# Second RMS norm of a decoder block: 1/rms on quarters of the partitions, rows through temporaries, small additions and two weight splits on GpSimd

## The chip, the cores and the metric

One core of one Trainium2 chip runs the whole block in one launch. The metric is device time in microseconds (us), less is better. Engines are named as the profile names them: PE is TensorE, DVE is VectorE, ACT is ScalarE, POOL is GpSimd, SP is SyncE, which issues nearly all DMAs here.

## What is computed

A decoder block over 512 tokens of 1024 features: an adaLN norm, an input projection, windowed attention and a short convolution, an output projection, then a second adaLN norm and a mixture of single-neuron experts (PEER). Only the join between the last two matters here:

```python
    x = x + gate1[:, None, :] * (merged @ w_out[l])
    h2 = modulate(rmsnorm(x, norm2_g[l]), shift2, scale2)     # (.. * rsqrt(mean(x*x)+eps) * g) * (1+scale2) + shift2
    x = x + gate2[:, None, :] * peer(h2, peer_wq[l], peer_subkeys[l], peer_u[l], peer_v[l])
# peer():
    q = (xt @ wq).reshape(T, PEER_HEADS, 2, PEER_HALF)        # 16 query blocks of 128 columns
    sc = jnp.einsum('thpd,hpkd->thpk', q, subkeys)            # scores against 128 keys per block
    vals, ids = lax.top_k(sc, PEER_TOPK)
```

## The kernel before

The activations lie transposed, features on the partitions: `xT` is 8 blocks of 128 features by 512 tokens. Every matmul that must be exact runs as three: weight and input are split into a hi part (written by ACT, rounded) and a lo part (the rest, `raw` minus `hi`, by DVE or POOL), and `mm3` adds hi·hi, hi·lo and lo·hi (lines 200, 201, 202). A block of weights is one DMA of 512 KB into `raw` (5 buffers), one ACT copy to `hi` (line 176) and one subtraction to `lo` (line 177).

The framework orders each engine's instructions when the program is built; on the chip every engine, and SP with its DMAs, works through its own list in order, and an instruction that waits holds up what stands behind it on its engine. Memory of a pool that is closed is given to the next pools, and an instruction that writes there waits for the last readers.

The place of the change, in order:

- Output projection, blocks 0 to 7 (`out_half`): 24 matmuls a block into `py`. DVE adds each block to `xT` (line 544), ACT squares it (line 221), DVE adds the squares up (line 223). Between them DVE works off the last columns of the adaLN matrix (`more_ada`, line 213, from DMA loads of 512 KB into two buffers), the last weights' lo parts, and `s2`, 1 + scale2 times the norm's gain (line 554).
- Sum over features: two matmuls with a matrix of ones into the bank `ss2` (lines 551 and 552). Every row of the result is the same: the sum for each of 512 tokens, repeated on 128 partitions. `rstd` takes the square root on ACT (line 241) and the reciprocal on DVE (line 242), both on 128x512.
- `spill`: 32 transposes of the new `xT` (line 532) into eight banks `xt`; ACT copies each to a row tile `xn` (line 535), and SP writes it to memory (`x1s`, line 536). The `xn` have three buffers.
- `modulated`, for each of 8 blocks: DVE makes `f` = xT·s2·r2 (line 229), ACT makes `fH` (line 230), DVE makes `fL` (line 231). PE runs the first two query blocks (`early`, 48 matmuls into `pq`) as blocks come in. Their weights are the first two of sixteen; the lo parts of these two are DVE's, those of the other fourteen POOL's.
- Two small additions a block put shift2 into 256 columns of `f` on ACT (lines 590 and 592); 16 transposes (`pg`, line 593) then give the token-major `hN` and `h2N`.
- For each of 16 query blocks: ACT copies the query out (`qs`), SP loads 64 KB of keys (`sk`, line 729, three buffers), PE makes the scores (`psc`, line 738), DVE takes the top sixteen. On PE the scores of block n stand ahead of the matmuls of block n+2.

The temporaries `tmp` (f, sq, rstd and others) are one set of 9 buffers of 128x512. After the transposes their memory goes to the pools of the next stage, in which `sk` and `qs` lie.

Of the kernel before, what the change touches and what calls it, by code (L numbers as in the profile page):

```python
# [7 lines left out]
F32 = mybir.dt.float32  # L8
# [5 lines left out]
AF = mybir.ActivationFunctionType  # L14
# [4 lines left out]
P = 128  # L19
T = 512  # L20
NCH = 4
D = 1024
DC = 8
ND = 3
TD = ND * P
HT = 32
TU = TD - HT
# [11 lines left out]
EARLY = 2  # L39
# [50 lines left out]
def body(tc, p):  # L90
    nc = tc.nc
# [6 lines left out]
    cp, cp_s = pool("cp")  # L98
# [5 lines left out]
    rt, rt_s = pool("rt", side="right")  # L104
    R2 = dict(tag="s2", bufs=3)
    tp, tp_s = pool("tp", side="right")
    T2 = dict(tag="t2", bufs=9)
    xp, xp_s = pool("xp", side="right")

    def bank(name):  # L110
        return psm.tile([P, 512], F32, tag="m", name=name)
# [55 lines left out]
    mark = [None]  # L167
# [24 lines left out]
    def weights_of(src, by=nc.vector):  # L192

        h, l = parts(src.rearrange("p a b -> p (a b)"), by)
        return (lambda k: h[:, k * P:(k + 1) * P]), (lambda k: l[:, k * P:(k + 1) * P])
# [20 lines left out]
    def tmp(name):  # L216
        return tp.tile([P, T], F32, name=name, **T2)

    def squared(b, so_far=None):
        q = tmp("sq")  # L220
        nc.scalar.activation(q, b, AF.Square)
        if so_far is not None:
            nc.vector.tensor_add(q, q, so_far)
        return q
# [9 lines left out]
    def square(ps, b, i, n, w=None):  # L234
        q = tmp("sq")
        nc.scalar.activation(q, b, AF.Square)
        nc.tensor.matmul(ps, ones if w is None else w, q, start=(i == 0), stop=(i == n - 1))

    def rstd(ps, n):
        r = tmp("rstd")  # L240
        nc.scalar.activation(r, ps, AF.Sqrt, scale=1.0 / n, bias=eps)
        nc.vector.reciprocal(r, r)
        return r
# [284 lines left out]
    def spill(half, when):  # L528
        for c in range(NCH):
            ps = bank("xt")  # L530
            for i in range(4):
                after(nc.tensor.transpose(ps[:, i * P:(i + 1) * P], xT[:, 4 * half + i, c * P:(c + 1) * P], ident),
                      when)
            xn = rt.tile([P, 512], F32, name="xn", **R2)
            nc.scalar.activation(xn, ps, AF.Copy)
            nc.sync.dma_start(x1s[c][:, half * 512:(half + 1) * 512], xn)

# [10 lines left out]
        if b < 6:  # L548
            more_ada(3)
    sq = squared(xT[:, 6, :], sq)  # L550
    nc.tensor.matmul(ss2, ones, sq, start=True, stop=False)
    end = nc.tensor.matmul(ss2, ones, squared(xT[:, 7, :]), start=False, stop=True)
    nc.vector.tensor_add(mod[:, 24:48], mod[:, 24:48], ab[:, 24:48])
    nc.vector.scalar_tensor_tensor(s2, mod[:, 32:40], 1.0, S("n2g"), op0=OP.add, op1=OP.mult)
    a1_s.close()
# [16 lines left out]
    hx, hx_s = pool("hx")  # L572
    fH = hx.tile([P, DC, T], F32R, name="fH")
    fL = hx.tile([P, DC, T], F32R, name="fL")
    r2 = rstd(ss2, D)
    spill(0, end)
    spill(1, end)
    early = [(weights_of(p["wq"][b]), bank("pq")) for b in range(EARLY)]
    fs = []
    for k in range(DC):  # L580
        fs.append(modulated(fH[:, k, :], fL[:, k, :], xT[:, k, :], r2, s2[:, k:k + 1], mod[:, 24 + k:25 + k]))
# [2 lines left out]
    for r, (dst, cs) in enumerate(((hN, slice(TD - P, TD)), (h2N, slice(TD, T)))):  # L584
        pg = [bank("pg0"), bank("pg1")]
        for k in range(DC):
            b = mod[:, 24 + k:25 + k]
            f = fs[k]
            if r == 0:
                nc.scalar.activation(f[:, TD - P:TU].rearrange("p (q t) -> p q t", t=HT),  # L590
                                     f[:, None, TU:TD].to_broadcast([P, P // HT - 1, HT]), AF.Identity, bias=b)
                nc.scalar.activation(f[:, TU:T], f[:, TU:T], AF.Identity, bias=b)
            nc.tensor.transpose(pg[k // 4][:, (k % 4) * P:(k % 4 + 1) * P], f[:, cs], ident)
        for k in range(2):
            nc.scalar.activation(dst[:, k * 512:(k + 1) * 512], pg[k], AF.Copy)
    xp_s.close()
# [535 lines left out]
```

## Time and profile before

| | us |
|---|---|
| three runs | 1437.29, 1440.34, 1440.64 (median 1440.34) |
| the profiled execution, its own time | 1436.58 |
| its span in the trace | 1434.8 |
| PE busy | 1385.5 (97%) |
| DVE busy | 1229.3 (86%) |
| ACT busy | 616.0 (43%) |
| POOL busy | 442.7 (31%) |

The span runs from the first to the last instruction of the trace; the 1.8 us beside it are start and end. Busy shares are averages over stages with different limits, so the change, which touches some 30 us around 214 to 260 us, has to be read in that stretch: who waits for whom there, and what the delay of one engine does to the next. PE's granted clock is 0.994 of full speed over the whole span.

### The profile page before, as it was taken

The numbers are of one execution on the slowest core, as the hardware profiler recorded it, in microseconds if no ns is written. First come the engines' busy times: TensorE is split into PE (matmuls) and PEld (weight loads), VectorE is DVE, ScalarE is ACT, GpSimd is POOL, SyncE is SP. The second block draws the span as 40 slices with busy tenths as digits, with TensorE's granted clock in tenths as the row PEclk, the third lists the DMA queues.
The fourth block names the chain that finished last, engine by engine and source line by source line (L and its number), as shares of the span: only waits on it lengthen the run. The fifth ranks groups of instructions, "written<-read, shape, count | busy, mean of one in ns | idle before, by whom it ended". The sixth has DMA issues, their size and how long they took to land.

```text
span 1434.8 us, 21241 instructions
## 1 busy us (share of the span) xinstructions
PE 1385.5 (97%) x7696; PEld 1218.7 (85%) x7696; DVE 1229.3 (86%) x2253; ACT 616.0 (43%) x1041; POOL 442.7 (31%) x306
## 2 busy tenths in 40 slices
PE   6999998999997999999999999999999999999998
PEld 4676776888997999999888888889999998889997
DVE  7778988789999999997668989888889979898964
ACT  4524645544634556463433333333344324333431
POOL 0000001440112320510134444456556556565400
PEclk9999999999999999999999999999999999999999
DMA  8645545322687997998999999999999999999843
GB/s 282 213 150 195 190 131 197 99 86 78 212 290 236 383 372 262 348 356 324 365 333 374 405 396 379 396 370 360 360 362 396 383 357 343 367 339 390 318 147 132
DMA packets 134376, 418.80 MB, mean 292 GB/s; under 512 B 12800, under 2 KB 39552, under 8 KB 132736
## 3 DMA queue, kind: packets, MB, share of 16 engines
q1 hardware_dynamic: 92800, 266.45, 51.6%
q0 software_dynamic: 41472, 151.01, 27.9%
q8 instruction: 60, 0.98, 0.3%
q14 instruction: 44, 0.36, 0.1%
HBM read 375.77 MB, written 41.62 MB: 291 GB/s over the span
## 4 chain that ended last, share of the span: by engine, by line
PE 62%; DVE 20%; DMA 8%; issue 7%; POOL 1%; ACT 1%; SPq 0%; DVEq 0%; POOLq 0%; ACTq 0%
PE o L997 10%; PE o L998 10%; PE o L996 10%; PE pa L200 5%; PE pa L202 5%; PE pa L201 5%; DVE lo L177 4%; DMA row<-in_vL,eG 3%; DMA ada<-in_ada 2%; PE pq L202 2%; PE pq L201 2%; PE pq L200 2%; DVE B L946 2%; DVE ga L912 2%; PE pj L200 2%
## 5 line engine op out<-in xcount | busy, mean ns | idle before, releaser
L176 ACT ACTIVATE hi<-raw 128x1024 fp32r<-128x1024 f32 x298 | 312.1, 1053 | 286.8 <-issue 91.4
L177 DVE TENSOR_TENSOR lo<-raw,hi 128x1024 fp32r<-128x1024 f32 x284 | 345.2, 1218 | 31.9 <-ACT hi L176 31.1
L202 PE MATMUL pa<-h2H,lo 128*128 128x352 f32 x1024 | 329.8, 322 | 5.6 <-DVE lo L177 5.5
L200 PE MATMUL pa<-h2H,hi 128*128 128x352 f32 x1024 | 332.3, 325 | 2.2 <-ACT sp L620 2.2
L201 PE MATMUL pa<-h2L,hi 128*128 128x352 f32 x1024 | 328.9, 321 | 0.0
L997 PE MATMUL o<-lo,wwh 128*128 128x512 f32 x768 | 299.2, 390 | 0.9 <-DVE lo L177 0.9
L996 PE MATMUL o<-hi,wwh 128*128 128x512 f32 x768 | 299.6, 390 | 0.0
L998 PE MATMUL o<-hi,wwl 128*128 128x512 f32 x768 | 298.8, 389 | 0.0
L776 POOL DMA_INDIRECT row<-in_uR,eG x128 | 186.7, 1459 | 321.3 <-PE o L998 187.8
L776 POOL DMA_INDIRECT row<-in_vL,eG x128 | 178.8, 1397 | 136.8 <-PE o L998 65.6
L784 DVE SCALAR_TENSOR_TENSOR junk<-row,h2N 128x1024 bf16<-128x1024 f32 x128 | 153.8, 1220 | 64.9 <-DMA row<-in_uR,eG 64.4
L202 PEld LDWEIGHTS pa<-h2H,lo 128*128 128x128 f32 x1024 | 192.7, 188 | 6.9 <-DVE lo L177 6.8
L200 PEld LDWEIGHTS pa<-h2H,hi 128*128 128x128 f32 x1024 | 192.2, 188 | 4.9 <-ACT sp L620 2.7
L201 PEld LDWEIGHTS pa<-h2L,hi 128*128 128x128 f32 x1024 | 192.5, 188 | 2.2
L912 DVE SCALAR_TENSOR_TENSOR ga<-row,av,ga 128x1024 f32<-128x1024 f32 x127 | 162.8, 1282 | 29.8 <-DMA row<-in_vL,eG 28.7
L998 PEld LDWEIGHTS o<-hi,wwl 128*128 128x128 f32 x768 | 144.2, 188 | 30.0
L997 PEld LDWEIGHTS o<-lo,wwh 128*128 128x128 f32 x768 | 144.2, 188 | 29.7 <-DVE lo L177 1.6
L996 PEld LDWEIGHTS o<-hi,wwh 128*128 128x128 f32 x768 | 144.2, 188 | 28.3 <-issue 0.2
L176 ACT ACTIVATE wwh<-w 128x768 fp32r<-128x768 f32 x64 | 54.1, 846 | 168.0 <-DVE w L979 120.8
L177 POOL TENSOR_TENSOR lo<-raw,hi 128x1024 fp32r<-128x1024 f32 x14 | 33.8, 2413 | 288.3 <-ACT hi L176 288.3
L978 ACT ACTIVATE w<-G 128x32 f32<-128x32 f32 x128 | 22.3, 221 | 191.3 <-DVE wwl L177 182.8
L776 POOL DMA_INDIRECT row<-in_uR,eH x32 | 43.2, 1350 | 161.7 <-DVE junk L784 74.5
(266 smaller groups left out, 1896.1 us busy)
## 6 DMA issues: line engine op xcount, KB each, us to landing
raw<-in_uL SPq DMA_DIRECT2D x128, 512.0 KB, 6.0
raw<-in_vL SPq DMA_DIRECT2D x128, 512.0 KB, 6.5
Gd<-st SPq DMA_DIRECT2D x12, 2048.0 KB, 10.2
G<-Gd SPq DMA_DIRECT2D x16, 1536.0 KB, 12.5
ada<-in_ada SPq DMA_DIRECT2D x32, 512.0 KB, 4.3
Ad<-sp SPq DMA_DIRECT2D x34, 352.0 KB, 6.5
sp<-Ad SPq DMA_DIRECT2D x34, 352.0 KB, 6.6
raw<-in_w_in SPq DMA_DIRECT2D x18, 512.0 KB, 5.2
```

The lines of the kernel that those rows point to most:

```text
L176: nc.scalar.activation(h, f, AF.Copy)
L177: by.tensor_sub(l, f, h.bitcast(F32))
L200: nc.tensor.matmul(ps, wh(k), rh(k), start=(k == k0), stop=False)
L201: nc.tensor.matmul(ps, wh(k), rl(k), start=False, stop=False)
L202: mark[0] = nc.tensor.matmul(ps, wl(k), rh(k), start=False, stop=(k == k1))
L776: d = nc.gpsimd.indirect_dma_start(out=t, out_offset=None, in_=tab, in_offset=bass.IndirectOffsetOnAxis(ap=e, axis=0))
L784: return nc.vector.scalar_tensor_tensor(junk, t, 1.0, h, op0=OP.mult, op1=OP.mult, accum_out=a)
L912: nc.vector.scalar_tensor_tensor(ga, t, av[:, k:k + 1], ga, op0=OP.mult, op1=OP.add)
L946: nc.vector.tensor_mul(B.rearrange("p t (h a b) -> p t h a b", h=8, a=4), H[:, ts, :, None, :].to_broadcast(sh), L[:, ts, None].to_broadca ...
L996: nc.tensor.matmul(o, wh[:, cs], vh[:, hs], start=(j == 0), stop=False)
L997: nc.tensor.matmul(o, wh[:, cs], vl[:, hs], start=False, stop=False)
L998: last = nc.tensor.matmul(o, wl[:, cs], vh[:, hs], start=False, stop=(j == NJ - 1))
```

## The change

It does five things, all around the second norm.

1. `grouped`: the sum over features is made by 4 matmuls of 128 tokens with 32 columns of ones instead of one of 512 tokens with 128. Quarter c of the tokens lands on partitions 32c to 32c+31, in the same 128 columns. So the root and the reciprocal run on 128x128. `spread` brings it back by 4 matmuls into a PSUM bank `rr`, from which DVE's line 229 reads. On PE the first 16 transposes of `spill` stand between the sum and `spread`.
2. The `xn` rows come from the temporaries, which are 13 buffers instead of 9.
3. The lo parts of the first two query blocks' weights go from DVE to POOL.
4. The 16 small additions go from ACT to POOL.
5. The 16 transposes `pg` are tied behind the early query matmuls.

```diff
-    T2 = dict(tag="t2", bufs=9)
+    T2 = dict(tag="t2", bufs=13)
...
+    def grouped(ps, q, first, last):
+
+        for c in range(NCH):
+            end = nc.tensor.matmul(ps[32 * c:32 * c + 32, 0:P], ones[:, 0:32], q[:, c * P:(c + 1) * P], start=first,
+                                   stop=last)
+        return end
+
+    def grouped_root(ps, n):
+        r = cp.tile([P, P], F32, tag="r", name="r", bufs=1)
+        nc.scalar.activation(r, ps[:, 0:P], AF.Sqrt, scale=1.0 / n, bias=eps)
+        nc.vector.reciprocal(r, r)
+        return r
+
+    def spread(r):
+
+        ps = psa.tile([P, 512], F32, tag="a", name="rr")
+        for c in range(NCH):
+            nc.tensor.matmul(ps[:, c * P:(c + 1) * P], ident[:, 32 * c:32 * c + 1].to_broadcast([P, P]), r,
+                             start=True, stop=True)
+        return ps
...
-            xn = rt.tile([P, 512], F32, name="xn", **R2)
+            xn = tmp("xn")
...
-    nc.tensor.matmul(ss2, ones, sq, start=True, stop=False)
-    end = nc.tensor.matmul(ss2, ones, squared(xT[:, 7, :]), start=False, stop=True)
+    grouped(ss2, sq, True, False)
+    end = grouped(ss2, squared(xT[:, 7, :]), False, True)
...
-    r2 = rstd(ss2, D)
+    r2 = grouped_root(ss2, D)
     spill(0, end)
+    r2 = spread(r2)
     spill(1, end)
-    early = [(weights_of(p["wq"][b]), bank("pq")) for b in range(EARLY)]
+    early = [(weights_of(p["wq"][b], nc.gpsimd), bank("pq")) for b in range(EARLY)]
...
             if r == 0:
-                nc.scalar.activation(f[:, TD - P:TU].rearrange("p (q t) -> p q t", t=HT),
-                                     f[:, None, TU:TD].to_broadcast([P, P // HT - 1, HT]), AF.Identity, bias=b)
-                nc.scalar.activation(f[:, TU:T], f[:, TU:T], AF.Identity, bias=b)
-            nc.tensor.transpose(pg[k // 4][:, (k % 4) * P:(k % 4 + 1) * P], f[:, cs], ident)
+                nc.gpsimd.tensor_scalar_add(f[:, TD - P:TU].rearrange("p (q t) -> p q t", t=HT),
+                                            f[:, None, TU:TD].to_broadcast([P, P // HT - 1, HT]), b)
+                nc.gpsimd.tensor_scalar_add(f[:, TU:T], f[:, TU:T], b)
+            after(nc.tensor.transpose(pg[k // 4][:, (k % 4) * P:(k % 4 + 1) * P], f[:, cs], ident), mark[0])
```

How the built program stands at three places follows; lines of the changed kernel have its own numbers.

The first place is SP's list behind the writes of the rows (`raw` from `in_wq` is the weights of a later query block, `sk` the keys, the brackets name the engines and queues waited for). Before:

```order
L536 DMA x1s_1651<-xn_1978 128x512 [waits DMAHW2_49,Activation_49]
L729 DMA sk_2133<-in_sk 128x128 [waits DMAHW3_49,DVE_49,PE_49]
L729 DMA sk_2137<-in_sk 128x128 [waits DMAHW4_49]
L729 DMA sk_2167<-in_sk 128x128 [waits DMAHW5_49]
L181 DMA raw_2681<-in_wq 128x1024 [waits DMAHW6_49,Pool_49]
L729 DMA sk_2248<-in_sk 128x128 [waits DMAHW7_49,DMAHW3_49,PE_49]
```

The same place of the changed kernel:

```order
L557 DMA x1s_1651<-xn_1989 128x512 [waits DMAHW2_49,Activation_49]
L181 DMA raw_2692<-in_wq 128x1024 [waits DMAHW3_49,Pool_49]
L751 DMA sk_2144<-in_sk 128x128 [waits DMAHW4_49,DMAHW2_49,DMAHW5_49,DMAHW1_49,DMAHW6_49,DMAHW0_49,DMAHW7_49,DVE_49,PE_49]
L751 DMA sk_2148<-in_sk 128x128
L751 DMA sk_2178<-in_sk 128x128
```

The first three loads of keys have moved behind a load of weights. Of the two waits that the list shows: the weights' wait for POOL is for the lo part of query block 4 in both programs; the first keys' wait for PE is for `xt`, the last transpose of `spill`, before (and DVE's for the last `f`), and for the last of the 16 `pg` transposes now.

The second place is ACT's list behind the sum, `r` or `rstd` being the root. Before:

```order
L241 ACTIVATE rstd<-ss_1652,eps 128x512
L535 ACTIVATE xn<-xt 128x512 x5
L230 ACTIVATE fH<-f,mod 128x512
L535 ACTIVATE xn<-xt 128x512
L230 ACTIVATE fH<-f,mod 128x512 x2
L535 ACTIVATE xn<-xt 128x512 x2
```

Changed:

```order
L248 ACTIVATE r<-ss_1652,eps 128x128
L556 ACTIVATE xn<-xt 128x512 x8
L230 ACTIVATE fH<-f,mod 128x512 x8
L176 ACTIVATE hi<-raw 128x1024
L777 ACTIVATE h2H<-fH 128x352
```

All eight row copies now stand ahead of the first `fH`; there were five.

The third place is DVE's list while the last two blocks of the output projection finish, with the two lo parts that leave it:

```order
-L553 TENSOR_TENSOR mod<-mod,sm 128x24
-L177 TENSOR_TENSOR lo<-raw,hi 128x1024
-L554 SCALAR_TENSOR_TENSOR s_104<-mod,sm 128x8
-L177 TENSOR_TENSOR lo<-raw,hi 128x1024
-L544 SCALAR_TENSOR_TENSOR xT<-py,mod,xT 128x512
+L574 TENSOR_TENSOR mod<-mod,sm 128x24
+L575 SCALAR_TENSOR_TENSOR s_104<-mod,sm 128x8
+L565 SCALAR_TENSOR_TENSOR xT<-py,mod,xT 128x512
```

Nothing else moved there; on POOL four lo parts, those of query blocks 0 to 3, now come ahead of the 16 additions, and the lo part of block 4 behind them.

## Rows read from the trace of the kernel before

**Rows 1.** Busy time by stretch: us (instructions) of each engine, PE clock, DMA share, GB/s.
```profile
260.00:350.00 90.00, 89.44 (x457) 76.02 (x456) 81.77 (x503) 35.34 (x72) 25.26 (x11) 1.00 0.30 92
420.00:500.00 80.00, 72.14 (x571) 71.14 (x570) 80.00 (x179) 37.16 (x67) 20.50 (x15) 0.96 0.84 302
```

**Rows 2.** Timeline of PE, 218 to 270 us: start, us, instruction, idle before it.
```profile
230.93 0.39 PE L202 MATMUL py<-mH,lo 128*128 128x512 f32 x1
...
234.08 1.12 PE L552 MATMUL ss<-sq,ones 128*128 128x512 f32 x2 [0.20 <-ACT sq L221]
235.04 3.66 PE L532 MATMUL xt<-cst,xT 128*128 128x128 f32 x32
241.74 0.73 PE L200 MATMUL pq<-fH,hi 128*128 128x512 f32 x2 [3.04 <-ACT fH L230]
...
253.19 1.91 PE L593 MATMUL pg<-cst,f 128*128 128x128 f32 x16
254.93 1.06 PE L738 MATMUL psc<-sk,qs 128*128 128x128 f32 x8
```

**Rows 3.** Timeline of ACT, 200 to 285 us.
```profile
214.86 1.06 ACT L176 ACTIVATE hi<-raw 128x1024 fp32r<-128x1024 f32 x1 [1.65 <-PE py L201]
...
233.39 0.63 ACT L221 ACTIVATE sq<-xT 128x512 f32<-128x512 f32 x1 [0.47 <-DVE xT L544]
...
239.85 1.23 ACT L535 ACTIVATE xn<-xt 128x512 f32<-128x512 f32 x2 [2.46 <-DMA x1s<-xn]
240.97 0.71 ACT L230 ACTIVATE fH<-f,mod 128x512 fp32r<-128x512 f32 x1
...
252.47 1.06 ACT L176 ACTIVATE hi<-raw 128x1024 fp32r<-128x1024 f32 x1 [0.34 <-PE pq L201]
```

**Rows 4.** Timeline of DVE, 200 to 290 us.
```profile
216.53 1.23 DVE L213 SCALAR_TENSOR_TENSOR junk<-ada,cact 128x1024 bf16<-128x1024 f32 x1 [0.57 <-DMA ada<-in_ada]
...
223.19 0.74 DVE L544 SCALAR_TENSOR_TENSOR xT<-py,mod,xT 128x512 f32<-128x512 f32 x1
...
225.93 0.18 DVE L553 TENSOR_TENSOR mod<-mod,sm 128x24 f32<-128x24 f32 x1
226.02 1.22 DVE L177 TENSOR_TENSOR lo<-raw,hi 128x1024 fp32r<-128x1024 f32 x1
227.16 2.36 DVE L554 SCALAR_TENSOR_TENSOR s<-mod,sm 128x8 f32<-128x8 f32 x1
...
232.62 0.75 DVE L544 SCALAR_TENSOR_TENSOR xT<-py,mod,xT 128x512 f32<-128x512 f32 x1
```

**Rows 5.** Timeline of POOL, 210 to 300 us.
```profile
226.89 2.60 POOL L177 TENSOR_TENSOR lo<-raw,hi 128x1024 fp32r<-128x1024 f32 x1 [226.44 <-ACT hi L176]
233.00 2.35 POOL L177 TENSOR_TENSOR lo<-raw,hi 128x1024 fp32r<-128x1024 f32 x1 [3.51 <-ACT hi L176]
253.60 2.37 POOL L177 TENSOR_TENSOR lo<-raw,hi 128x1024 fp32r<-128x1024 f32 x1 [18.26 <-ACT hi L176]
```

**Rows 6.** Reciprocals on DVE (lines 242 and 501), small copies on ACT (line 741): ns min/median/max.
```profile
L242 DVE RECIPROCAL rstd<-rstd x5: 3344/3353/3353, 15.7 to 236.0; 128x512 f32<-128x512 f32 x5
L501 DVE RECIPROCAL rq<-rq x1: 353/353/353, 87.5 to 87.5; 128x32 f32<-128x32 f32 x1
L741 ACT ACTIVATE scg<-psc x16: 274/279/335, 256.7 to 347.8; 128x128 f32<-128x128 f32 x16
```

**Rows 7.** Timeline of SP, 205 to 290 us.
```profile
256.00 0.33 SPq L181 DMA_DIRECT2D raw<-in_wq  x1
256.43 0.37 SPq L729 DMA_DIRECT2D sk<-in_sk  x1
```

**Rows 8.** Key loads to landing: the one of 256.43 us, then all 16.
```profile
DMA to landing us min/median/max: 3.3/3.3/3.3
...
DMA to landing us min/median/max: 1.7/1.8/3.3
```

**Rows 9.** A short instruction among POOL's groups by line: busy us, mean ns.
```profile
L1124 POOL MEMSET const-uint8-127<- 128x1 uint8 x1 | 0.1, 119 | 0.0
```

## The prediction

> **What bounds the kernel now.** I read busy time by stretch first. From 260 to 350 us PE is busy 89.44 of 90 us, from 420 to 500 us DVE 80.00 of 80 [rows 1]. DVE's input in the first stretch is scores that PE makes, so if PE comes out of the second norm later, everything behind comes later by as much: I carry the change's balance one to one to the end. PE's timeline shows where it stands still around the norm [rows 2]. The last product of the output projection ends at 231.32. The second half of the sum starts at 234.08, behind ACT's square of the last block (233.39 to 234.02, [rows 3]), and ends at 235.20. Transposes fill 235.04 to 238.70, then PE idles 3.04 us for `fH` until 241.74. From there to 253.19 it runs the early queries, 48 matmuls in 11.45 us. The 16 `pg` transposes follow, the first scores start at 254.93, and PE goes on without a pause. So there are two places to read: 231 to 242 us, which the change is about, and 253 to 255 us, which it also touches.
>
> **Part 1, two lo parts on POOL.** DVE loses two instructions of some 1.15 us ahead of the last two `xT`; the one of 226.02 is one [rows 4]. But POOL's lo is not free for DVE. In this trace one two-operand DVE instruction out of SBUF meets a POOL lo: `s2`, 8 columns. It starts at 227.16 and takes 2.36 us, to 229.52 [rows 4], while POOL's lo ends at 229.49; that lo took 2.60 where the others take 2.35 and 2.37 [rows 5], and it began under DVE's own lo, which ran to 227.24. I read this as each shutting out the other until it is done. `xT` at 232.62, with one operand in PSUM, ran 0.75 us beside the POOL lo of 233.00, as long as the 0.74 of 223.19: no such wait.
>
> The Trainium skill, page "SBUF — State Buffer", section "Who interferes with whom", says that a DVE instruction with two SBUF inputs and a GpSimd instruction that reads SBUF exclude each other, whole instruction by whole instruction. The row of `s2` agrees with 2.36 us; by this rule the term below is +1.0, without it −1.1.
>
> Now the order of events with that wait. `hi` of query block 0 ends at 215.92 [rows 3]; POOL's lo holds from 216.0 to 218.37. DVE's adaLN column of 216.53 is shut out and ends about 219.5 instead of 217.7. Then `xT` (0.75) ends at 220.25, ACT's square and next `hi` (0.63, 1.06) at 222.0; DVE meanwhile does a column, an addition and a lo of its own (1.15, 0.61, 1.15) until 223.1. POOL's second lo then runs to 225.47, the next column to 226.6, `xT` of block 5 to 227.35, where it was 223.93 [rows 4]. From there POOL's third lo is asked for after a square and a `hi`, 1.74 us later; DVE needs 1.15 + 0.61 + 0.18 for column, addition and `mod` and is done 1.87 us later. So POOL goes first again, and `s2` waits until 227.35 + 1.87 + 2.37 = 231.6. `xT` of block 6 ends at 232.3, its square and addition (0.63, 0.69) at 233.7, `xT` of block 7 at 234.4, the last square at 235.0. Before it was 234.02: **+1.0**. If there were no such wait, block 7's product (231.32), ACT's `hi` ahead of the square (1.06, by then to 232.3) and the square (0.63) would set it: 232.9, or −1.1. I take +1.0, since the one row of such a meeting shows the whole wait.
>
> **Part 2, sum, root, spreading.** Four matmuls of 128 columns cost like `psc`'s four: 0.82 to 0.88 us from the first to the next work [rows 2], against 1.12: I take 0.95 with the end of the pipe, −0.1. If the four went side by side it would be one of them, 0.2: −0.8. (The Trainium skill, page "TensorEngine Tiling (Array Packing)", says that tiles of 32 columns can run in parallel; that is the −0.8 end. No row here shows it.) I count from the sum's end. The root at the rate of 128x128 copies takes 0.3 [rows 6]; the reciprocal, between 0.35 for 32 columns and 3.35 for 512, 0.95: ready at 1.3. PE is in the first 16 transposes until 1.83 (3.66 for 32), so the reciprocal's 2.4 us saving ends there. `spread` takes to 2.75, the other 16 transposes to 4.55. All eight `xn` stand ahead of `fH` on ACT now, so the last is copied (0.6) by 5.3 and `fH` (0.71) is done at 6.0. Before, this was 241.74 − 235.20 = 6.54: **−0.5**. What is saved in the DMA wait of 2.46 us ahead of 239.85 [rows 3] goes back to three more copies in front.
>
> **Part 3, the additions on POOL.** ACT had room for them; on POOL their 96 and 160 columns cost 0.22 and 0.38 us at the lo's rate (2.37 for 1024). DVE's `fL` reads two operands of SBUF, so some of them wait for such an addition, up to 0.38 each; DVE has three `f` ready before `fH` exists and is ahead of PE later. I put **+0.2** on the 11.45, from 0 to 1.5.
>
> **Part 4, the first keys.** This is the largest term. SP now loads weights for block 8 ahead of the first keys. That load waits for POOL's lo of block 4, which waits for `hi`, which waits for nearly the last early matmul. This chain is in the trace as it stands [rows 3, 5, 7]: `hi` 252.47, lo 253.60 to 255.97, the load at 256.00, keys behind it at 256.43, on PE's clock 0.72 us before to 3.24 us after 253.19. Only nothing waited for those keys, the fourth. Now the first keys have that place. They landed after 3.3 us [rows 8], at 259.73, and PE's scores stand ahead of the next queries, so what started at 254.93 starts 4.8 us later. Bounds: without the weights in front, the keys would still wait for the last `pg` transpose (254.93) and take the usual 1.8: +1.8. I take **+4.8**, since the row is the same pair of loads.
>
> Part 5, tying `pg` behind the early matmuls, costs nothing: they stood there already.
>
> **Sum**: 1.0 − 0.1 − 0.5 + 0.2 + 4.8 = +5.4 us. The profiled execution took 1436.58 (span 1434.8), so 1442.0; the median of the three runs lies 3.8 above that execution, and I predict its counterpart, 1440.34 + 5.4 = 1445.7.
>
> **Rivals.** *No shutting out, so not slower.* If the 2.36 us of `s2` had another cause, part 1 gives −1.1 and the sum is +3.3: 1443.6, which is no change by the measure of 0.3%, 4.3 us, about what a measurement of this kernel can tell. It decides as soon as part 1 is below −0.1. For it: it is one row; against it: the ends agree within 0.03 us.
> *The keys come early.* If the key loads don't wait behind the weights' data, or a later stretch takes up the pause (DVE, not PE, is full from 420 us), part 4 shrinks to 1.8 or less: +2.4 or down to about −1, 1439 to 1442.7. Against it: DVE's list there starts from the scores, and PE has 0.56 us idle in 90 us to catch up with.
> *POOL is too slow for the additions.* They start after the first `fL`, 0.8 us into the early queries, and have 10.9 us for 16. At over 0.68 us each they hold up `pg`, the lo of block 4 and with it the keys; at 1.0 it is +5.1, 1450.8. For it: a lo of 2.4 us is all that POOL shows of arithmetic, and each second addition waits for the first; against it: a memset of one column takes 0.12 [rows 9].
>
> **Chances.** Forecast (+4.3 to +7.5) 0.55, no shutting out 0.2, keys early or taken up 0.15, slow additions 0.1. Slower by over 0.3%: most of the first, the last, a little of the second, 0.6; same 0.36; faster 0.04, which needs the third with the −1.1 and more. The forecast's own range is 1444 to 1448; to hold 8 in 10 it reaches into the second and third cases and the slow additions' lower part: 1440.5 to 1450.
>
> **What would show it.** DVE instructions of adaLN columns or `s2` of 2 to 3 us beside POOL lo parts near 217, 224 and 230 us; the last square ending about 235.0; root and reciprocal near 0.3 and 0.95; `fH` first at 5.3 us behind the sum, right after the eighth `xn`; additions of 0.2 to 0.4 us; and above all PE idle for some 4.7 us before `psc`, waiting for the DMA of `sk`, with SP's load of weights waiting for POOL just ahead. I am wrong if that pause is missing, or if PE's early queries start over 2 us before 241.7.

## The result, and the profile after

The changed kernel took 1449.70 us (median of five runs, 1447.86 to 1453.62), the kernel before 1440.34 beside it: 0.84% slower by the ratio on record, 1.0084 with a 95% interval of 1.0062 to 1.0106 (the two medians alone give 1.0065). Run again later beside the kernel before it was 1.0081 (1.0050 to 1.0113). The forecast had +5.4 us; the medians give +9.4, the two ratios, taken of 1440 us, 12.1 and 11.7. So the direction was right, the time lies just inside the upper end of the range, and the change that was forecast is about half of the measured one.

The profiled execution of the changed kernel took 1449.7 us (span 1447.9), 13.1 more than the one before. I compare the two by distances from the end of the last matmul of the output projection, because what lies ahead of it has nothing to do with the change and still came 3.5 us earlier in this execution (227.79 in place of 230.93 + 0.39 = 231.32, [rows 2]).

Busy time by stretch of the changed kernel, columns as in [rows 1]:

```profile
260.00:350.00 90.00, 89.70 (x440) 75.89 (x441) 77.53 (x482) 33.21 (x68) 24.11 (x11) 0.97 0.28 87
420.00:500.00 80.00, 72.04 (x543) 71.15 (x543) 79.93 (x191) 35.79 (x65) 21.66 (x15) 0.96 0.82 285
230.00:237.00 7.00, 6.10 (x41) 5.58 (x34) 1.43 (x4) 3.39 (x6) 2.32 (x1) 0.53 0.55 193
256.00:260.30 4.30, 0.00 (x1) 0.03 (x1) 0.00 (x0) 1.64 (x3) 2.39 (x2) 0.70 0.50 168
260.30:264.20 3.90, 3.90 (x13) 3.49 (x14) 1.25 (x9) 0.66 (x2) 0.00 (x0) 0.50 0.50 155
```

The first two rows answer to [rows 1]: PE still bounds one stretch and DVE the other. The other three are new. PE's granted clock, the third number from the right, is 0.53 from 230 to 237 us and 0.50 from 260.3 to 264.2, that is its lower level (1.2 GHz); before, it was 1.00 in the same part. In between PE does nothing at all for 4.3 us.

PE's timeline of the changed kernel, which answers to [rows 2]:

```profile
227.40 0.39 PE L202 MATMUL py<-mH,lo 128*128 128x512 f32 x1
229.72 0.43 PE L242 MATMUL ss<-sq,ones 128*32 128x128 f32 x8 [1.94 <-DVE sq L223]
231.05 0.65 PE L242 MATMUL ss<-sq,ones 128*32 128x128 f32 x8 [0.90 <-ACT sq L221]
231.63 3.68 PE L553 MATMUL xt<-cst,xT 128*128 128x128 f32 x16
235.10 1.92 PE L256 MATMUL rr<-r,cst 128*128 128x128 f32 x8
236.81 2.12 PE L553 MATMUL xt<-cst,xT 128*128 128x128 f32 x16
240.37 0.73 PE L200 MATMUL pq<-fH,hi 128*128 128x512 f32 x2 [1.45 <-ACT fH L230]
...
251.81 1.02 PE L615 MATMUL pg<-cst,f 128*128 128x128 f32 x7
253.78 1.20 PE L615 MATMUL pg<-cst,f 128*128 128x128 f32 x9 [0.94 <-POOL f L614]
260.30 2.04 PE L760 MATMUL psc<-sk,qs 128*128 128x128 f32 x8 [5.31 <-DMA sk<-in_sk]
...
268.77 1.05 PE L760 MATMUL psc<-sk,qs 128*128 128x128 f32 x8
```

The first 16 transposes behind the sum take 3.68 us, the last 16 2.12; before, all 32 took 3.66. The first scores (`psc`) take 2.04 us in place of 1.06, after a pause of 5.31 us for the keys, and the second scores start 8.47 us behind the first in place of 6.41. Set against the sum of the prediction, with the rows before from their timelines:

| stretch on PE's path | before | after | forecast | measured |
|---|---|---|---|---|
| last product to end of last square | 2.70 | 3.21 | +1.0 | +0.5 |
| to end of the sum | 1.18 | 0.70 | -0.1 | -0.5 |
| to first early query matmul | 6.54 | 8.67 | -0.5 | +2.1 |
| to first `pg` transpose | 11.45 | 11.44 | +0.2 | 0.0 |
| to first scores | 1.74 | 8.49 | +4.8 | +6.75 |
| to second scores | 6.41 | 8.47 | 0 | +2.1 |
| sum | 30.0 | 41.0 | +5.4 | +11.0 |

POOL, answering to [rows 5] and [rows 9]:

```profile
212.48 2.38 POOL L177 TENSOR_TENSOR lo<-raw,hi 128x1024 fp32r<-128x1024 f32 x1 [212.04 <-DVE sq L223]
218.31 3.43 POOL L177 TENSOR_TENSOR lo<-raw,hi 128x1024 fp32r<-128x1024 f32 x1 [3.45 <-ACT hi L176]
...
241.20 1.54 POOL L612 TENSOR_SCALAR f<-f,mod 128x96 f32<-128x96 f32 x1 [8.88 <-DVE fL L231]
...
252.43 0.52 POOL L612 TENSOR_SCALAR f<-f,mod 128x96 f32<-128x96 f32 x1
253.05 0.68 POOL L614 TENSOR_SCALAR f<-f,mod 128x160 f32<-128x160 f32 x1
253.70 2.35 POOL L177 TENSOR_TENSOR lo<-raw,hi 128x1024 fp32r<-128x1024 f32 x1
...
397.57 1.56 POOL L798 DMA_INDIRECT row<-in_uR,eH  x1 [67.65 <-DMA raw<-in_uL]
```

DVE, answering to [rows 4] and to the reciprocal of [rows 6]:

```profile
212.82 3.12 DVE L213 SCALAR_TENSOR_TENSOR junk<-ada,cact 128x1024 bf16<-128x1024 f32 x1 [0.42 <-DMA ada<-in_ada]
...
219.48 3.34 DVE L213 SCALAR_TENSOR_TENSOR junk<-ada,cact 128x1024 bf16<-128x1024 f32 x1
...
225.37 2.25 DVE L575 SCALAR_TENSOR_TENSOR s<-mod,sm 128x8 f32<-128x8 f32 x1
...
232.17 0.95 DVE L249 RECIPROCAL r<-r 128x128 f32<-128x128 f32 x1 [1.69 <-ACT r L248]
```

ACT, answering to [rows 3], and SP with the landing of the first three key loads, answering to [rows 7] and [rows 8]:

```profile
231.77 0.37 ACT L248 ACTIVATE r<-ss,eps 128x128 f32<-128x128 f32 x1 [0.77 <-PE ss L242]
...
251.14 1.06 ACT L176 ACTIVATE hi<-raw 128x1024 fp32r<-128x1024 f32 x1 [2.67 <-PE pq L201]
...
254.64 1.08 ACT L617 ACTIVATE h2N<-pg 128x512 f32<-128x512 f32 x2
255.60 1.11 ACT L753 ACTIVATE qs<-pq 128x512 f32<-128x512 f32 x2
```

```profile
256.08 0.33 SPq L181 DMA_DIRECT2D raw<-in_wq  x1
256.71 1.28 SPq L751 DMA_DIRECT2D sk<-in_sk  x3
```

```profile
DMA to landing us min/median/max: 2.6/2.9/3.1
```

Read from the bottom: the keys are issued at 256.71 because the weights ahead of them are issued at 256.08; these wait for POOL's lo of 253.70 to 256.05; and that began 1.5 us behind its `hi` (251.14 + 1.06) because POOL was still at the additions, 0.52 and 0.68 us each. On ACT the query copies (`qs`) stand behind four copies of `pg`.

### The profile page after: what moved, and what is told of

It is laid out like the page before. It is cut to its first block, busy times and chain, and to the rows that moved or that the text cites. A ratio compares the mean times of both kernels' runs of the same rounds, so it can differ in the third digit from the quotient of the medians.

```text
span 1447.9 us, 21293 instructions
## 1 busy us (share of the span) xinstructions
PE 1392.4 (96%) x7716; PEld 1225.7 (85%) x7716; DVE 1228.4 (85%) x2251; ACT 611.1 (42%) x1025; POOL 468.6 (32%) x324
## 4 chain that ended last, share of the span: by engine, by line
PE 55%; DVE 19%; DMA 13%; issue 8%; POOL 4%; ACT 1%; SPq 0%; DVEq 0%; POOLq 0%; ACTq 0%
PE pa L202 7%; PE pa L200 7%; PE pa L201 7%; PE o L1020 6%; PE o L1019 6%; DMA row<-in_uR,eG 6%; PE o L1018 6%; DVE lo L177 4%; POOL row L798 3%; DVE junk L213 2%; DVE junk L806 2%; DMA row<-in_vL,eG 2%; DMA ada<-in_ada 2%; PE pq L200 2%; PE pq L202 2%
## 5 line engine op out<-in xcount | busy, mean ns | idle before, releaser
L798 POOL DMA_INDIRECT row<-in_uR,eG x128 | 190.8, 1490 | 321.4 <-PE o L1020 170.9
L798 POOL DMA_INDIRECT row<-in_vL,eG x128 | 182.7, 1427 | 132.4 <-PE o L1020 65.1
L177 POOL TENSOR_TENSOR lo<-raw,hi 128x1024 fp32r<-128x1024 f32 x16 | 39.3, 2457 | 268.8 <-DVE sq L223 212.0
```

The costliest lines, as they stand in the source:

```text
L177: by.tensor_sub(l, f, h.bitcast(F32))
L798: d = nc.gpsimd.indirect_dma_start(out=t, out_offset=None, in_=tab, in_offset=bass.IndirectOffsetOnAxis(ap=e, axis=0))
```

## The experiments

Twelve more runs were made, one of them of the changed kernel again, each beside the kernel before. Ratios are to the kernel before, with 95% intervals. The other columns are read from each run's timelines, as in the table above: PE's pause ahead of the sum, whether the granted clock stayed at 1.00 in the sum and the transposes, and the distances on PE's path (early is from the first query matmul to the first `pg` transpose). The intervals of the changed kernel, fill, lo_dve, adds_act and fill_one overlap; between these the distances in the traces speak and not the times.

| kernel | pause | clock kept | sum's end to `pq` | early | `pg` to scores | to second scores | last product to second scores | ratio |
|---|---|---|---|---|---|---|---|---|
| before | 1.43 | yes | 6.54 | 11.45 | 1.74 | 6.41 | 30.0 | 1 |
| changed | 1.94 | no | 8.67 | 11.44 | 8.49 | 8.47 | 41.0 | 1.0084 (1.0062 to 1.0106) |
| after_again | 1.94 | no | 8.66 | 11.45 | 8.01 | 8.68 | 40.7 | 1.0081 (1.0050 to 1.0113) |
| keys_first | 1.17 | in part | 7.35 | 11.45 | 4.05 | 8.11 | 34.1 | 1.0048 (1.0032 to 1.0064) |
| sum_plain | 1.19 | yes | 5.71 | 12.11 | 8.19 | 8.05 | 37.7 | 1.0041 (1.0025 to 1.0058) |
| fill | filled | yes | 5.98 | 11.45 | 7.90 | 8.49 | 37.6 | 1.0066 (1.0042 to 1.0091) |
| lo_dve | 1.37 | yes | 5.98 | 11.44 | 8.34 | 8.35 | 37.2 | 1.0058 (1.0037 to 1.0080) |
| adds_act | 1.95 | no | 8.63 | 11.49 | 6.99 | 9.12 | 40.2 | 1.0055 (1.0035 to 1.0075) |
| tmp9 | 1.20 | yes | 4.39 | 13.39 | 1.89 | 6.40 | 29.0 | 0.9988 (0.9970 to 1.0006) |
| before_tmp13 | 1.22 | yes | 5.71 | 12.88 | 7.40 | 8.18 | 37.8 | 1.0034 (1.0016 to 1.0052) |
| fill_one | 1.95 | no | 6.34 | 11.43 | 8.03 | 9.11 | 39.9 | 1.0091 (1.0065 to 1.0118) |
| keys_adds_fill | filled | yes | 5.98 | 11.47 | 3.66 | 6.51 | 31.4 | 1.0021 (1.0003 to 1.0038) |
| best | filled | yes | 4.52 | 11.74 | 1.75 | 6.40 | 27.9 | 0.9996 (0.9978 to 1.0014) |
| before_late | 1.96 | no | 5.84 | 13.19 | 1.74 | 6.41 | 32.8 | 1.0001 (0.9978 to 1.0024) |

### The pause ahead of the scores

keys_first:

```diff
+    def key(hp):
+        sk = hx.tile([P, P], F32, tag="sk", name="sk", bufs=3)
+        nc.sync.dma_start(sk, p["sk"][hp])
+        return sk
+
+    keys = [key(hp) for hp in range(3)]
     fs = []
...
-        sk = rp.tile([P, P], F32, tag="sk", name="sk", bufs=3)
+        sk = keys[hp] if hp < 3 else key(hp)
...
-        nc.sync.dma_start(sk, p["sk"][hp])
```

> The changed kernel, with one difference: the first three loads of keys go to tiles that do not lie over the temporaries, and are issued before the weights of a later query block, so nothing holds them up. Theory: the pause of 5.3 us ahead of the first scores is the keys' alone, and the lower clock that follows it (scores at 2.04 us, matmuls every 0.43 us) comes from that pause. Then scores start 1.7 to 3 us behind the start of the pg transposes in place of 8.5, the granted clock stays 1.00 there, and the time falls by some 7 us, to 1442 to 1443. Rival 1: the additions on POOL hold up the query copies as well, so the scores still start 4 us or more behind pg: 1446. Rival 2: a later stage, where DVE or the row transfers bound, takes up what is saved: 1449.

Rival 1 in part. PE's timeline of keys_first:

```profile
253.34 1.20 PE L622 MATMUL pg<-cst,f 128*128 128x128 f32 x9 [0.65 <-POOL f L621]
255.82 1.73 PE L766 MATMUL psc<-sk,qs 128*128 128x128 f32 x8 [1.28 <-ACT qs L759]
```

The keys account for 4.4 of the 8.5 us. What is left, 4.05, waits for the additions on POOL (0.65) and for the query copies on ACT, and the clock falls in this shorter stop as well: 0.57 from 256 to 260 us.

adds_act puts the additions back on ACT, both of each block alike:

```diff
...
-                nc.gpsimd.tensor_scalar_add(f[:, TU:T], f[:, TU:T], b)
...
+                nc.scalar.activation(f[:, TU:T], f[:, TU:T], AF.Identity, bias=b)
```

> The changed kernel with the 16 additions back on ACT. Theory: the additions on POOL took 0.65 us each on the average, kept POOL until 253.7 us, and so put off the lo part of block 4, the load of weights that waits for it, and the keys behind that load. With them on ACT that lo part begins right behind its hi part, about 1.6 us earlier against pg, pg doesn't wait for POOL, and the scores start 6.5 to 7 us behind the start of pg in place of 8.5; the time falls by 1.5 to 2 us against the changed kernel. Rival: pg's copies and the query copies set the start, not POOL: 8 us or more, no change.

As the theory had it: 6.99 us. The weights are issued 2.85 us behind the start of `pg` (4.27 in the changed kernel, 2.81 before). So the additions cost 1.4 to 1.5 us of the pause.

tmp9:

```diff
-    T2 = dict(tag="t2", bufs=13)
+    T2 = dict(tag="t2", bufs=9)
...
-            xn = tmp("xn")
+            xn = rt.tile([P, 512], F32, name="xn", **R2)
```

> The changed kernel with 9 temporaries again and the rows xn in their own three buffers; everything else of the change stays. In its program the first keys stand ahead of the weights for block 8 on SP again, and one query copy (qs) stands ahead of the pg copies on ACT. Theory: the whole of the pause ahead of the first scores, with the slow clock behind it, comes from the 13 temporaries, by two moves that they make: keys behind weights on SP, and query copies behind the pg copies on ACT. Then scores start about 2 us behind the start of pg (1.74 before, plus some 0.7 that the additions on POOL hold up pg), the second scores 6.4 us later, and the time is within 3 us of before: 1438 to 1441. Rival: the moves are not the only cause, the lo part of block 4 behind the additions on POOL holds the keys' successors too; then a second pause shows at the scores of block 2 or 3, and it is 1442 to 1444.

The theory held: 1.89 us from `pg` to the scores, no low clock, and the whole loss is gone. No second pause came, although the lo parts and the additions were on POOL. Two things went along with it. The pause ahead of the sum was 1.20 us here, not 1.94, so that the loss behind the sum went too; with 13 temporaries keys_first and sum_plain had such short ones as well, so this part is not shown to be the temporaries'. And with the first `fH` ahead of most row copies again, the first query matmul comes after 4.39 us, but the early queries, which wait for ACT in between, take 13.39 us in place of 11.45. The reverse, before_tmp13, puts that part alone on the kernel before (the diff of tmp9 with its signs turned):

> The kernel before with one part of the change alone: 13 temporaries, the rows xn among them. Theory: this part alone puts the first keys behind the weights for block 8 on SP and the query copies behind the pg copies on ACT, and so makes the pause: scores 6.8 to 7.1 us behind the start of pg (6.99 in the changed kernel with the additions on ACT), slow clock behind them, second scores 8.5 to 9.1 us later in place of 6.4. At the sum it gains 0.8 us (5.7 us from the sum's end to the first query matmul, as with the plain sum in the changed kernel). Together 6.5 to 7.5 us slower than before: 1445 to 1446.5. Rival: the pause needs the lo parts or the additions on POOL as well; then it is within 2 us of before.

7.40 and 8.18 us, 0.34% slower in place of the 0.45 to 0.5% expected: the 13 temporaries alone make the pause. The clock fell at one more place in this run, behind PE's pause of 2.21 us ahead of `pq`, and the early queries took 12.88 us. keys_adds_fill is the changed kernel with the edits of keys_first, adds_act and fill (below) together:

> The changed kernel with three parts undone at once: first keys loaded early into tiles of their own, additions on ACT, and the three idle matmuls ahead of the sum. What is left of the pause is then the query copies' place behind the pg copies on ACT. Theory: pg doesn't wait, its last copy ends about 1 us behind it, the query copies follow, and the scores start 3.2 to 3.5 us behind the start of pg (4.05 with the additions on POOL, 1.74 before); from the last product to the second scores 31 to 32 us (30.0 before, 41.0 in the changed kernel), a little more if the clock falls in the shorter pause. Time: 0 to 2 us above before, 1439 to 1441. Rival: something else holds the scores; then it is 1442 or more.

3.66 us, of which PE waits 1.75 for `qs`; the clock stays at 1.00, and 31.4 us to the second scores. What is left is the query copies' place on ACT.

### The clock behind the sum

sum_plain takes `rstd` and the two 512-column matmuls of before, in the changed kernel.

```diff
-    grouped(ss2, sq, True, False)
-    end = grouped(ss2, squared(xT[:, 7, :]), False, True)
+    nc.tensor.matmul(ss2, ones, sq, start=True, stop=False)
+    end = nc.tensor.matmul(ss2, ones, squared(xT[:, 7, :]), start=False, stop=True)
...
-    r2 = grouped_root(ss2, D)
+    r2 = rstd(ss2, D)
     spill(0, end)
-    r2 = spread(r2)
```

> The changed kernel with the sum over features by two 512-column matmuls, root and reciprocal on 128x512 as before, no spreading. Theory: the transposes behind the sum ran at half speed (3.68 us for 16) because the four 128-column matmuls leave PE nearly idle for 3 us ahead of them and the granted clock falls to its lower level; with 512-column matmuls the clock stays 1.00 there and 32 transposes take 3.7 us. The reciprocal costs 3.35 us again, so from the sum's end to the first query matmul 6 to 6.5 us where it is 8.7: about 2 us less, 1447.7. Rival: it is the longer wait for the last squares (two lo parts on POOL) that lowers the clock, whatever the sum's form: transposes stay slow, and the time is 1449 to 1451.

The transposes took 3.66 us again. But the pause ahead of the sum was 1.19 us here, not 1.94, so it didn't separate the two theories. The 5.71 us look better than the 5.98 of the grouped sum at full clock (fill, lo_dve), but they are no gain: from the end of the last square to the first `pg` transpose the plain sum takes 1.18 + 5.71 + 12.11 = 19.0 us, the grouped one in lo_dve 0.48 + 5.98 + 11.44 = 17.9.

fill:

```diff
+    idle = psa.tile([P, 512], F32, tag="a", name="idle")
+    last = mark[0]
+    for i in range(2):
+        after(nc.tensor.matmul(idle, ones, xT[:, i, :], start=True, stop=True), last)
-    grouped(ss2, sq, True, False)
+    half = grouped(ss2, sq, True, False)
+    after(nc.tensor.matmul(idle, ones, xT[:, 2, :], start=True, stop=True), half)
```

> The changed kernel with three 512-column matmuls of no use in the idle time of PE ahead of the sum: two behind the last product, one between the sum's halves. Theory of the clock: with PE busy there the granted clock stays 1.00, 16 transposes take 1.83 us, the spreading 0.9, and the first query matmul starts 6 us behind the sum's end, as the prediction had it; the whole is 2 to 2.7 us faster, 1447 to 1447.7. Rival: the transposes are slow for another reason (row writes, banks, the partitions of the sum); then nothing moves, or the sum starts up to 0.5 us later: 1449.7 to 1450.2.

The mechanism is right: clock 1.00, 16 transposes in 1.97 us, and 5.98 us to the first query matmul. The whole is 1448.03 in place of the 1447 to 1447.7 expected, within what the runs scatter; the ratio, 1.0066 against 1.0084, doesn't show the gain, the trace does.

lo_dve:

```diff
-    early = [(weights_of(p["wq"][b], nc.gpsimd), bank("pq")) for b in range(EARLY)]
+    early = [(weights_of(p["wq"][b]), bank("pq")) for b in range(EARLY)]
```

> The changed kernel with the two lo parts back on DVE. Theory: POOL's lo parts shut DVE's two-operand instructions out (3.1 and 3.3 us for columns of 1.23), so that the last square came some 0.5 us later against the last product than before; with them back the columns take 1.23 us again, the last square ends 2.7 us behind the last product in place of 3.2, and the time falls by 0.5 us, less than these runs can tell: 1449. Rival: DVE was relieved by as much as it was shut out, or more; then the last square comes at the same distance or later, 1449.7 to 1450.8. If the wait ahead of the sum is what lowers PE's clock, the transposes get faster here too, and it is 1447.

The adaLN columns take 1.23 us again, the square ends 2.64 us behind the last product, and with a pause of 1.37 us the clock stays up.

after_again is the changed kernel without an edit.

> The changed kernel itself once more, as a control beside the other three. It tells which parts of its first trace repeat: the scores 8.5 us behind the start of pg should stand again within 0.3 us; the half-speed transposes behind the sum may or may not (in four relatives of it they came once in full and twice not at all, where a matmul of 512 columns or a later last product lay ahead). If they repeat, the first query matmul starts 12 to 12.6 us behind the last product, else 9.1 to 10. Time: 1447 to 1451.

The half-speed transposes stand again (3.68 us), with the pause of 1.94 us. The scores came 8.01 us behind `pg`, outside the 0.3 us that I had given it. fill_one then takes only the filler between the sum's halves:

```diff
-    grouped(ss2, sq, True, False)
+    idle = psa.tile([P, 512], F32, tag="a", name="idle")
+    half = grouped(ss2, sq, True, False)
+    after(nc.tensor.matmul(idle, ones, xT[:, 2, :], start=True, stop=True), half)
```

> The changed kernel with a single idle 512-column matmul, between the sum's halves, where PE stood idle for 0.90 us; the pause ahead of the first half stays. Theory: the clock falls because the grouped halves, 0.43 us each, leave PE nearly idle for over 3 us, so one matmul of 1.1 us in the middle is enough, as the plain sum's first half was: granted clock 1.00, 16 transposes 1.97 us, 6.0 us from the sum's end to the first query matmul. Rival: the 1.94 us of idle time ahead of the first half is what lowers it, and the filler comes too late: transposes 3.3 to 3.7 us as in the changed kernel. If the pause ahead is only 1.2 us in this run (it was 1.94 in four programs with the lo parts on POOL, 1.2 in three), the run tells little. Time against the changed kernel: 2.7 us less or the same.

The rival held. Timeline of PE and busy time by stretch in fill_one:

```profile
231.03 0.43 PE L242 MATMUL ss<-sq,ones 128*32 128x128 f32 x8 [1.95 <-DVE sq L223]
231.38 2.08 PE L574 MATMUL idle<-xT,ones 128*128 128x512 f32 x2
233.39 0.66 PE L242 MATMUL ss<-sq,ones 128*32 128x128 f32 x8
233.98 2.32 PE L553 MATMUL xt<-cst,xT 128*128 128x128 f32 x16
```

```profile
229.00:231.00 2.00, 0.08 (x1) 0.00 (x0) 1.31 (x3) 1.38 (x2) 0.00 (x0) 1.00 0.50 145
231.00:234.00 3.00, 2.97 (x19) 0.89 (x19) 0.79 (x3) 0.83 (x2) 2.35 (x1) 0.56 0.22 83
```

After 1.95 us of nothing the filler itself runs at the lower level, 2.08 us in place of 1.12. So my theory of the short grouped matmuls fell, and before_late asks whether the plain sum of before is any safer. It holds DVE up by one instruction:

```diff
     sq = squared(xT[:, 6, :], sq)
+    nc.vector.tensor_tensor(sq, sq, sq, op=OP.max)
```

> The kernel before with one DVE instruction more: behind the sum of squares up to block 6 it takes the larger of that tile and itself (128x512, two operands, about 0.69 us by the addition of the same shape; no value changes). The plain sum of 512 columns thus starts some 2.0 us behind the last product in place of 1.43, and the last block's xT and square come 0.6 us later too. Theory from fill_one: the length of PE's pause ahead of the sum decides the clock, whatever the sum's form; with 2 us it falls to 0.5 in the sum, its second half takes 1.9 us and more in place of 1.12, and the 32 transposes 5 us or more in place of 3.66, and the first query matmul starts 2 us or more later. Rival: it is the grouped halves, too short to hold the clock; then the plain sum keeps it at 1.00, the transposes take 3.66 us, and only some 0.6 us are lost. Time: 1 to 3 us above before by the theory, 0.5 by the rival; the traces decide.

PE and busy time by stretch in before_late:

```profile
233.56 2.03 PE L552 MATMUL ss<-sq,ones 128*128 128x512 f32 x2 [1.96 <-DVE sq L551]
235.39 1.85 PE L553 MATMUL ss<-sq,ones 128*128 128x512 f32 x2
237.08 3.66 PE L532 MATMUL xt<-cst,xT 128*128 128x128 f32 x32
```

```profile
231.00:233.00 2.00, 0.60 (x3) 0.18 (x1) 1.27 (x3) 1.57 (x2) 0.00 (x0) 1.00 0.60 168
234.00:237.00 3.00, 3.00 (x4) 0.87 (x4) 0.32 (x3) 0.63 (x1) 1.72 (x1) 0.50 0.40 127
```

It isn't: a pause of 1.96 us lowers the clock ahead of the plain sum too, although its longer matmuls work through most of the low stretch, so that the transposes run at 3.66 us again (I had expected 5 or more). It takes 2.8 us more to the second scores, 1.2 of them in the sum and 1.7 in the early queries, where the clock was low again from 243.9 to 247.3 us, behind PE's pause of 2.35 us ahead of `pq`; the ratio, 1.0001 with 0.0023 to either side, can't show that. In all, the clock fell in the sum in all five profiles with an unfilled pause of 1.94 to 1.96 us, and in one (keys_first) of the six with 1.17 to 1.43. The length is not all that counts. PE's pause ahead of `pq` left the clock at 1.00 with 3.04 us in the kernel before [rows 2] and with 2.22 in sum_plain, and lowered it with 2.21 in before_tmp13 and 2.35 in before_late. Ahead of the first scores 1.28 us lowered it in keys_first, and 1.75 in keys_adds_fill did not. What decides there stays open.

### A version from the parts

best keeps the grouped sum with the filler, puts lo parts and additions back, goes back to 9 temporaries, moves the first two weight splits ahead of the second half of `spill`, and gives the rows six buffers of their own:

```diff
...
-            xn = tmp("xn")
...
+            xn = hx.tile([P, 512], F32, tag="xn", name="xn", bufs=6)
...
     spill(0, end)
+    write()
     r2 = spread(r2)
...
+        if k == 1:
+            write()
```

`write` issues the row copies that `spill` has left open, so four come behind the second block's `f`.

> A version put together from the parts: the grouped sum with its spreading, three idle 512-column matmuls of PE ahead of and in it, 9 temporaries, the rows xn in six buffers of their own, their last four copies issued behind the second block's f so that ACT does the first fH ahead of three of them; lo parts on DVE and additions on ACT as before. Keys ahead of weights and one query copy ahead of the pg copies, as before. Theory: from the sum's end, rr at 2.75, f at 3.4, fifth row copy to 4.3, first fH at 4.9, first query matmul 5.0 us behind the sum's end where it was 6.54 before; nothing is given back at pg and the scores: 1.5 us faster than before, a gain that is about as large as these runs can tell. Rival: the early queries, which ACT and DVE then feed later against PE, last 1 us longer or more (row copies in between), and it is the same as before within 0.5 us.

On PE's path it did what it should: 4.52 us from the sum's end, 27.9 to the second scores, 2.1 less than before. The time is 0.9996 of before, with 0.0018 (2.6 us) to either side; so a gain is not shown.

## Why the prediction came out as it did

**Right.** Part 4's mechanism, the largest term: PE stood still ahead of `psc` for the DMA of `sk`, the weights' load waiting for POOL's lo just ahead, and taking out the 13 temporaries alone takes away the pause and the low clock behind it. Part 1's pattern: the columns took 3.12 and 3.34 us and `s2` 2.25 beside POOL's lo parts. Root 0.37, reciprocal 0.95, first `fH` right behind the eighth `xn`; and where the clock stayed up, 5.98 us from the sum's end, for a forecast of 6.0.

**Part 1, +1.0.** It was +0.5 in six profiles with the lo parts on POOL (3.21 or 3.22 us from last product to last square), and -0.2 to -0.3 in three others (2.44 to 2.47). The shutting out goes either way round: where DVE's column starts first, POOL's lo takes 3.44 us instead. I had let POOL go first each time. The Trainium skill, page "SBUF — State Buffer", section "Who interferes with whom", says that the ports DVE shares with GpSimd are an exclusive lock and that the order of issue decides who blocks; the trace agrees, by 3.12 us on the one side and 3.43 on the other.

**Part 2, -0.1 and -0.5.** The sum's two halves went side by side: eight records of 0.43 us, the end that I had at -0.8; measured -0.5, and -0.7 in lo_dve and tmp9, where the clock stayed up. (The Trainium skill, page "TensorEngine Tiling (Array Packing)", section "Key Properties", says that different tiles can execute in parallel; 0.43 us for four matmuls agrees, against the 1.06 of `psc` [rows 2].) The -0.5 behind the sum stood, at full clock. At the lower level it was 8.67 - 5.98 = 2.7 us worse.

**The step that failed is that the sum took every duration of PE at the clock of before.** What part 1 adds to PE's pause, forecast as 1.0 us and measured as 0.5, it priced by its length alone. With 1.94 us in place of 1.43 the clock fell, and cost 2.7 us behind the sum; in the pause that part 4 makes, which the sum had at 4.8 us with nothing behind it, it fell again and cost 2.1 us behind the first scores (6.51 and 6.40 us to the second ones in keys_adds_fill and tmp9, where it stayed up). These 4.75 us are most of the 5.6 that the forecast lacked at the second scores. At the place itself the trace before says 1.00. Elsewhere it did warn: [rows 1] has 0.96 between 420 and 500 us, where the clock was 0.50 from 441.7 to 448.5 us, from the middle of a pause of PE of 6.99 us on, and three shorter stretches of 0.50 lie ahead of 125 us.

**Part 3, +0.2.** Its size was wrong and its place too. Undisturbed, the additions took 0.52 and 0.68 us, not 0.22 and 0.38: going from 96 to 160 columns adds 0.16, so by estimate about 0.28 lie in each whatever its length, which the rate of the lo part can't show. Five of the sixteen, all beside an `fL` of DVE, took longer, 0.79 to 1.54; I had put that wait on DVE's side. At the 1.27 us of an undisturbed pair all would take 10.2 us, to 251.4 by estimate, ahead of the end of `hi` (252.20); they took 12.5. From 241.20 to 253.73 they kept POOL until behind the early queries. These didn't get longer, but the lo of block 4 came 1.5 us later and with it the keys. That is the third rival, which I had given 0.1, half true beside the first case.

**Part 4, +4.8.** Measured +6.75, of which 1.4 to 1.5 are part 3's, 0.2 a longer gap between weights and keys, and 0.3 a longer way from there to the first scores. I had also overlooked the second hold-up, the query copies behind the `pg` copies: it is covered by the keys' wait, and would have left 3.66 us with the keys in time.

**Not in the forecast at all: the first row fetch.** In the changed kernel POOL issues the first fetch of expert rows 67.65 us behind its last work, in place of 64.32 before (the last row of POOL's timeline above). DVE is 2.1 us later for it at the second fetch's product (404.90 against 395.42, +9.5, where it was +7.4 ahead). DMA queues of the changed kernel from 395 to 397.6 us, with packets, MB and share of the 16 engines:

```profile
q1 hardware_dynamic: 164, 0.61, 72.8%
q14 instruction: 2, 0.02, 1.5%
```

Two loads of instructions (q14) fall there; the first begins 2.03 us ahead of the fetch. Counted from the second scores, the fetch is late by 3.3 and 3.8 us in the two profiles of the changed kernel, by 3.8 in keys_first, 3.6 in fill and 2.4 in fill_one, which all keep every part of the change; each of these has a load of instructions that begins 2.0 to 2.3 us ahead of the fetch. In sum_plain, lo_dve and adds_act, with one part undone, the fetch comes after 64.3 us, with the load 2 us behind it or long before. A program whose list on POOL is longer meets its load at another place; that fits, but no run moved the load alone, and tmp9, with a load 2.25 us ahead, lost only 0.1, so it is argued and not shown.

With it, 11.0 and 2.1 make 13.0 us from the last product on in the profiled pair; -3.5 ahead of it and +3.6 near 680 us (where PE's clock is 0.91 from 660 to 700 us and was 1.00) make up the rest of the 13.1. The first of these differs from execution to execution: the last product ended anywhere from 227.8 to 232.6 us in the fourteen timelines. The second isn't the change's either: before_late, without any part of it, loses the same 3.6 us there, and the clock was low for some us between 672 and 692 us in every profile except that of the kernel before. after_again, which lost about 1 us there, takes 13.3 us more than before from the last product to the end of the span, 10.7 of them up to the second scores. The rival "a later stage takes up the pause" got no support: +7.43 us at 268 us was +7.43 at 390.

## What to carry to other kernels

A buffer count is a change of order: more temporaries moved the keys behind a blocked load on one engine's list and the query copies behind others on another's, and cost more than everything else here; so read the order of every queue around a buffer that is reused. When a change lets PE pause longer, price the work behind the pause at the lower clock as one case, even if the trace before shows full speed there. And price a small instruction on GpSimd by one of its own size: a long one says nothing of what each costs at least.

## What the runs showed of the hardware that was not expected

- PE's granted clock fell from 1.00 to 0.50 behind an unfilled pause of 1.94 to 1.96 us ahead of the sum in five profiles of five, and behind one of 1.17 to 1.43 in one of six. Ahead of `pq` it fell behind 2.21 and 2.35 us, and not behind 2.22 and 3.04. It stayed low while PE worked without a stop, as at 0.50 from 260.3 to 264.2 us in the changed kernel.
- Four matmuls of 128 columns on 32 columns of the array each took 0.43 us together at full clock, 0.65 where it fell.
- An addition on POOL of 96 columns took 0.52 us, of 160 columns 0.68, where its lo part of 1024 took 2.35; beside an `fL` of DVE it took up to 1.54.
- The first fetch of rows came 2.4 to 3.8 us later in every program in which a load of instructions began some 2 us ahead of it and all parts of the change stood; tmp9 had such a load 2.25 us ahead and lost 0.1.
